# Band attention with each tile's transposes behind the next tile's scores, two key buffers in the first differential part, and row factors sent through DRAM

## The chip, the cores and the metric

The kernel runs on one core of a Trainium2 chip. A core has a matrix engine (TensorE, PE in the profile; its weight loads are listed as PEld), a vector engine (VectorE, DVE), a scalar engine (ScalarE, ACT), a general engine (GpSimd, POOL) and a queue engine (SyncE, SP) that issues all of this kernel's DMAs. Each engine takes its instructions in order; they wait for each other through semaphores. Matrix products are written to PSUM, of which this kernel uses eight banks; everything else on the core lies in SBUF, and DRAM holds inputs, outputs and scratch. The metric is the device time of one execution in microseconds, as a median of several runs.

## The reference

One inference step of a one-layer encoder for 2048 prompt tokens and 32 sample tokens, width 1024. What matters here:

```python
z = rmsnorm(x, g_attn) @ w_in             # columns: qa ka va | qb kb vb
# group A: 4 heads, differential, two maps of 64 dims each, 128-wide values
s = q·k / 8 + t5_bias,  masked by 64-token chunks
w = softmax(s_map0) - lam * softmax(s_map1);   oa = w @ v
# group B: 8 heads of 64; a 64-token chunk sees itself and the 8 chunks before it
s = q·k / 8 + clip_bias;   ob = softmax(s) @ v
h = x + concat(rmsnorm(oa) * (1 - lam_init), rmsnorm(ob)) @ w_out
h = h + relu(rmsnorm(h) @ w_up)**2 @ w_down
y = rmsnorm(h + sigmoid(h @ w_ple_gate) * (p @ w_ple_proj))
```

The keys and values of both groups are outputs too. The sample tokens run the same layer against caches of 128 rows.

## The kernel before

Products are made from numbers split in a high and a low part of a short float type (`split`), three matmuls for one product in `mm3` (lines 215 to 217). Tokens go in four blocks `b` of 512 (the last has the 32 sample tokens as well), and blocks in two halves, 0 and 1, 2 and 3.

*Preparation.* `prep` takes a block in tiles of 128 tokens: load, sum of squares on ScalarE, eight transposes into two PSUM tiles `xp`, copies out of them into the high and low activations, a copy `xt` that is written to DRAM as `xT`, and the row factor 1/rms (`rsqrt`, into one column of `rcol`). The activations are not multiplied by that factor; it is applied to the products. The value projection needs it per partition (`rcol`, line 421). The query and key projections have tokens along the free axis, so they need it as a row that is the same on all partitions: `rb[b]`, tile name `rbt`. Lines 390 to 392 make it for each tile, by a transpose of the broadcast column into a PSUM tile `rp` and a copy by ScalarE. `rp` takes its PSUM buffer from the same small rings as `xp` and, for blocks 2 and 3, as the projections (`mm`, two buffers).

*Projection.* `proj` makes values (`vtile`), then for each head group queries and keys, and writes them to DRAM scratch (`qS`, `kS`, `vS`). Lines 475 and 480 read `rb`.

*Differential attention.* `attn_a(js, ...)` runs over four heads; for a head it loads the bias tile `ba`, the keys `kt` (tile name `ka`) and then for each pair `j` of query tiles calls `attn_a_pair`, which loads queries, makes the scores (line 632), exponentials, transposes (704) and products with values (718 to 720). It is used twice: for blocks 0 and 1 (`self.small`, pool `a0`), where `ka` has one buffer of 1024 columns, and later for blocks 2 and 3, where it has two.

*Band attention.* `attn_b(js, ...)` runs over eight heads and is called for four groups of pairs: (0,1), (2,3), (4,5) and (6,7,8), pair 8 being the sample tokens. A head's bias `bb`, keys `kbt`, queries `q` and values `vbt` are loaded first. `attn_b_pair` then does, for each of the pair's two tiles of 128 queries: scores into PSUM tiles `sb` (line 802, up to 640 keys, in two pieces where there are more than 512), bias and running maximum on VectorE into `eb` (805, four buffers), exponential with its sum (810) and scaling (812) on ScalarE, transposes into `tpb` (817), and copies into a high and a low part `pHb` (826, ScalarE) and `pLb` (827, VectorE). After both tiles come the products with the values `ob` (842), two copies (846, 847) and, once a head, a store to `oT`.

*What sets the order.* The kernel is written with a tile framework that simulates the program and from it lays out one order for each engine:

```python
with tile.TileContext(nc, schedule_with_timeline_sim=True) as tc:
```

Among the instructions that are ready in that simulation, and whose buffers are free, the one that stands first in the program is taken. An instruction far down the program may thus run early where those before it wait; on the chip the order is then fixed. `lifted` gives the preparation of blocks 2 and 3 the rank of the place where the first differential part begins. In `run` the order of the parts is: preparation of blocks 0 and 1 with group A's values, group A's queries and keys for that half, `attn_a` for blocks 0 and 1, group B's projections for blocks 0 and 1 with the preparation of block 2, `attn_b` for pairs 0 to 3, group B's projections for block 2 with the preparation of block 3, and for block 3, `attn_b` for pairs 4 to 8, and then the second half of group A, output projection and MLP.

Of the kernel before, what the change touches and what calls it, by code (L numbers as in the profile page):

```python
# [15 lines left out]
ALU = mybir.AluOpType  # L16
# [126 lines left out]
class Kern:  # L143
# [214 lines left out]
    def prep(self, b, acts, pp, mm, tag, first=None):  # L358
        nc = self.nc
        aH, aL = acts[b]  # L360
        for i, (c0, n) in enumerate(toks(b)):
            t0 = 512 * b + c0
            x = pp.tile([P, D], F32, tag="x", name="x")
            self.dma(x[:n], self.xsrc(t0, n))
            if first is not None:
                first()
                first = None
            xt = pp.tile([P, 8, P], F32, tag="xt", name="xt")
            st = pp.tile([P, 1], F32, tag="st", name="st")
            nc.scalar.activation(  # L370
                xt[:n].rearrange("p a b -> p (a b)"), x[:n], AF.Square, accum_out=st[:n]
            )
            for h in range(2):
                xp = mm.tile([P, 4, P], F32, tag=tag, name="xp")
                for k in range(4):
                    kk = 4 * h + k
                    nc.tensor.transpose(xp[:, k, :n], x[:n, kk * P : kk * P + P], self.ident[:n, :n])
                for k in range(4):
                    kk = 4 * h + k
                    g = self.g_attn[:, kk : kk + 1]  # L380
                    hi, lo = aH[:, kk, c0 : c0 + n], aL[:, kk, c0 : c0 + n]
# [4 lines left out]
                nc.vector.tensor_copy(xt[:, 4 * h : 4 * h + 4, :n], xp[:, :, :n])  # L386
# [4 lines left out]
            nc.tensor.transpose(rp[:, :n], r.broadcast_to([n, P]), self.ident[:n, :n])  # L391
            nc.scalar.activation(self.rb[b][:, c0 : c0 + n], rp[:, :n], AF.Copy)
            yield

    def ktok(self, b):
# [374 lines left out]
    def attn_b_pair(self, h, j, kt, v, kb, bb, q, t1, pool, ps_s, ps_t, ps_o):  # L770
        nc = self.nc
        samp = j is None
        if samp:
# [4 lines left out]
        pH = pool.tile([P, 6, 256], F32R, tag="pH", bufs=2, name="pHb")  # L778
        pL = pool.tile([P, 6, 256], F32R, tag="pL", bufs=2, name="pLb")
        spans = []  # L780
        for qi, t in enumerate(tiles):
            if samp:
                nr, k0, n, b0 = SS, SP, PAST + SS, 384
                kts = [(0, P), (1, SS)]
            else:
                nr = P
                f = max(0, t - 4)
                k0, n = P * f, P * (t + 1 - f)
                b0 = 640 - n
                kts = [(i, P) for i in range(f, t + 1)]  # L790
            spans.append(kts)
            if n <= 512:
                nb, w = 1, n
            else:
                nb, w = 2, n // 2
            e = pool.tile([P, 640], F32, tag="e", bufs=4, name="eb")[:nr, :n]
            st = pool.tile([P, 5], F32, tag="st", bufs=4, name="stb")[:nr]
            for i in range(nb):
                s = ps_s.tile([P, 512], F32, tag="s", name="sb")[:nr, :w]
                for hl in range(2):  # L800
                    c = k0 - kb + w * i
                    nc.tensor.matmul(
                        s, q[:, hl, P * qi : P * qi + nr], kt[:, c : c + w], start=hl == 0, stop=hl == 1
                    )
                nc.vector.tensor_tensor_reduce(
                    e[:, w * i : w * i + w], s, bb[:nr, b0 + w * i : b0 + w * i + w], 1.0, -3e38,
                    ALU.add, ALU.max, st[:, 3 + i : 4 + i],
                )
            nc.vector.tensor_reduce(st[:, 0:1], st[:, 3 : 3 + nb], axis=AX.X, op=ALU.max, negate=True)
            nc.scalar.activation(e, e, AF.Exp, bias=st[:, 0:1], accum_out=st[:, 1:2])  # L810
            nc.vector.reciprocal(st[:, 2:3], st[:, 1:2])
            nc.scalar.activation(e, e, AF.Copy, scale=st[:, 2:3])
            for x0 in range(0, len(kts), 4):
                ch = kts[x0 : x0 + 4]
                tp = ps_t.tile([P, 4, P], F32, tag="tp", name="tpb")
                for x, (i, kn) in enumerate(ch):
                    nc.tensor.transpose(  # L817
                        tp[:kn, x, :nr], e[:, P * (x0 + x) : P * (x0 + x) + kn], self.ident[:nr, :nr]
                    )
                groups = [(0, len(ch), P)] if not samp else [(0, 1, P), (1, 1, SS)]  # L820
                for a0, na, kn in groups:
                    sl = ch[0][0] - kfirst + a0
                    h_ = pH[:kn, sl : sl + na, P * qi : P * qi + nr]
                    l_ = pL[:kn, sl : sl + na, P * qi : P * qi + nr]
                    s_ = tp[:kn, a0 : a0 + na, :nr]
                    nc.scalar.activation(h_, s_, AF.Copy)
                    nc.vector.tensor_tensor(l_, s_, h_.bitcast(F32), op=ALU.subtract)
        o = ps_o.tile([P, 256], F32, tag="o", name="ob")
        order = []
        if samp:  # L830
            order = [(0, P, 0, nq), (1, SS, 0, nq)]
        else:
# [5 lines left out]
            order += [(i, P, 128, 256) for i in s1 if i not in s0]  # L838
        for x, (i, kn, qa, qb) in enumerate(order):
            vt = v[:kn, (SP - kb) // P + i] if samp else v[:kn, i - kb // P]  # L840
            for y, pt in enumerate((pH, pL)):
                nc.tensor.matmul(  # L842
                    o[:, qa:qb], vt, pt[:kn, i - kfirst, qa:qb],
                    start=x == 0 and y == 0, stop=x == len(order) - 1 and y == 1,
# [725 lines left out]
```

## Time and profile before

| | us |
|---|---|
| median of 3 runs | 3191.57 (3189.75 to 3192.46) |
| the profiled execution | 3197.78 |
| its span, first to last instruction | 3196.0 |
| TensorE busy in the span | 3037.6 |
| ScalarE, GpSimd, VectorE busy | 1885.5, 1887.4, 1851.6 |
| mean granted TensorE clock | 0.977 |

A line of a group of instructions names the source line, the engine, the operation and the tiles written and read, then how often it ran, its busy time, the mean duration of one, and the idle time of the engine before it with what ended it. A line of a wait reads "engine, tile, line <- what it waited for: total us, times, longest". A line of a timeline starts with the time from the span's start and the duration; brackets hold the idle time before it and its releaser. A stage's line has its time, then busy time and number of instructions of PE, PEld, DVE, ACT and POOL, the granted clock, the DMA engines' mean busy share and their rate. Busy times of matmuls include overlap in the pipeline, so that the distance from start to start says what one costs in a row of many.

### The profile page before, as it was taken

To read this page: it belongs to the slowest core of one execution; us is meant where nothing else is said; L and a number is where in the kernel's file an instruction comes from. 1 tells how busy PE (TensorE), PEld (TensorE's weight loads), DVE (VectorE), ACT (ScalarE), POOL (GpSimd) and SP (SyncE) were. 2 spreads that over 40 slices of the span, in tenths; PEclk is the share of its full clock that TensorE was granted. 3 is DMA by queue.
4 is the path that set the end of the run, shared out by engine and by line. 5 is a ranking of instruction groups with operands and counts; after the bars stand their busy time and mean duration, and the time that the engine had idled before them with its cause. 6 is when DMAs were issued, how large, how long until landed. Compare 5 with 4: busy or idle time off the path is not lost.

```text
span 3196.0 us, 53414 instructions
## 1 busy us (share of the span) xinstructions
PE 3037.6 (95%) x18265; PEld 2694.5 (84%) x18265; DVE 1851.6 (58%) x4448; ACT 1885.5 (59%) x4166; POOL 1887.4 (59%) x2572
## 2 busy tenths in 40 slices
PE   8998989999999998999999999998999999899998
PEld 7787877899987787877788888877888888899998
DVE  5157774544454554666765666435577665776663
ACT  5256775766665764676665666554555555554445
POOL 4466546333335544565554555677787778867674
PEclk9998999999999999999999999999999999999999
DMA  8787767977688745555554534446524334233331
GB/s 267 237 242 224 208 191 237 251 227 206 199 244 227 209 130 134 149 165 138 170 158 139 148 111 119 126 147 216 182 86 147 106 99 127 93 100 108 92 114 55
DMA packets 512505, 521.61 MB, mean 163 GB/s; under 512 B 37949, under 2 KB 393601, under 8 KB 512233
## 3 DMA queue, kind: packets, MB, share of 16 engines
q1 hardware_dynamic: 512232, 518.19, 55.2%
q8 instruction: 145, 2.38, 0.3%
q14 instruction: 128, 1.04, 0.1%
HBM read 412.08 MB, written 109.95 MB: 163 GB/s over the span
## 4 chain that ended last, share of the span: by engine, by line
PE 68%; DMA 12%; DVE 10%; ACT 4%; issue 3%; POOL 2%; SPq 1%; DVEq 0%; ACTq 0%; POOLq 0%
PE dps L215 6%; PE dps L216 6%; PE dps L217 6%; PE ups L215 6%; PE ups L216 6%; PE ups L217 6%; PE s L632 3%; PE qps L215 3%; PE qps L216 3%; PE qps L217 3%; DMA oraw<-oT 2%; PE ob L842 2%; PE tpb L817 1%; PE tpp L704 1%; DMA wr<-w_up 1%
## 5 line engine op out<-in xcount | busy, mean ns | idle before, releaser
L175 POOL TENSOR_TENSOR wl<-wr,wh 128x256 fp32r<-128x256 f32 x648 | 474.5, 764 | 333.6 <-ACT wh L180 328.0
L180 ACT ACTIVATE piece<-wr 128x512 fp32r<-128x512 f32 x412 | 252.9, 626 | 289.0 <-PE ups L216 144.0
L175 POOL TENSOR_TENSOR piece<-wr,piece 128x256 fp32r<-128x256 f32 x416 | 336.4, 834 | 103.2 <-ACT piece L180 87.8
L180 ACT ACTIVATE wh<-wr 128x1024 fp32r<-128x1024 f32 x228 | 240.8, 1057 | 198.5 <-PE qps L216 51.7
L165 POOL TENSOR_TENSOR wl<-wr,wh 128x256 fp32r<-128x256 f32 x264 | 197.9, 781 | 185.8 <-ACT wh L180 180.4
L215 PE MATMUL ups<-cs,piece 128*128 128x256 f32 (+1 forms) x896 | 257.3, 288 | 7.8 <-ACT piece L180 6.1
L217 PE MATMUL ups<-cs,piece 128*128 128x256 f32 (+1 forms) x896 | 257.4, 287 | 5.6 <-POOL piece L175 5.6
L216 PE MATMUL ups<-cs,piece 128*128 128x256 f32 (+1 forms) x896 | 256.6, 286 | 0.5 <-DVE cs L186 0.5
L216 PE MATMUL dps<-ul,piece 128*128 128x272 f32 (+1 forms) x768 | 247.7, 324 | 1.3 <-DVE ul L186 1.3
L217 PE MATMUL dps<-uh,piece 128*128 128x272 f32 (+1 forms) x768 | 247.5, 324 | 1.2 <-POOL piece L165 1.2
L215 PE MATMUL dps<-uh,piece 128*128 128x272 f32 (+1 forms) x768 | 246.2, 324 | 1.0 <-DVE h L1124 0.8
L165 POOL TENSOR_TENSOR piece<-wr,piece 128x256 fp32r<-128x256 f32 x280 | 223.5, 829 | 25.1 <-ACT piece L180 24.3
L1124 DVE TENSOR_TENSOR h<-h,dps 128x272 f32<-128x272 f32 (+1 forms) x384 | 190.8, 515 | 81.5 <-PE dps L217 80.5
L215 PE MATMUL qps<-aH,wh 128*128 128x512 f32 (+1 forms) x640 | 230.8, 361 | 5.8 <-DVE ql L475 4.3
L215 PE MATMUL dps<-uh,wh 128*128 128x512 f32 x512 | 209.5, 409 | 20.8 <-ACT wh L180 7.2
L216 PE MATMUL qps<-aL,wh 128*128 128x512 f32 (+1 forms) x640 | 229.2, 358 | 0.0
L217 PE MATMUL qps<-aH,wl 128*128 128x512 f32 (+1 forms) x640 | 228.4, 357 | 0.0
L1083 DVE TENSOR_TENSOR h<-h,dps 128x512 f32<-128x512 f32 x256 | 174.2, 682 | 82.3 <-PE dps L217 77.6
L632 PE MATMUL s<-ka,q 128*128 128x512 f32 (+3 forms) x768 | 188.6, 349 | 19.4 <-DMA ka<-kS 10.0
L215 PE MATMUL ups<-cH,wh 128*128 128x512 f32 x512 | 202.7, 396 | 0.5 <-DVE h L1083 0.4
L216 PE MATMUL dps<-ul,wh 128*128 128x512 f32 x512 | 202.1, 395 | 0.0
L217 PE MATMUL dps<-uh,wl 128*128 128x512 f32 x512 | 202.1, 395 | 0.0
(298 smaller groups left out, 9764.7 us busy)
## 6 DMA issues: line engine op xcount, KB each, us to landing
wr<-w_up SPq DMA_DIRECT2D x128, 512.0 KB, 4.1
wr<-w_down SPq DMA_DIRECT2D x128, 512.0 KB, 3.7
wr<-w_in SPq DMA_DIRECT2D x74, 512.0 KB, 4.6
q<-qS SPq DMA_DIRECT2D x128, 256.0 KB, 5.2
v<-vSa SPq DMA_DIRECT2D x64, 512.0 KB, 3.9
ka<-kS SPq DMA_DIRECT2D x32, 512.0 KB, 7.8
wr<-w_out SPq DMA_DIRECT2D x32, 512.0 KB, 5.0
wr<-w_ple_gate SPq DMA_DIRECT2D x32, 512.0 KB, 4.1
```

The costliest lines, as they stand in the source:

```text
L165: nc.gpsimd.tensor_tensor(out[:, sl], a[:, sl], b[:, sl], op=op)
L175: nc.gpsimd.tensor_tensor(out[:, sl], a[:, sl], b[:, sl], op=op)
L180: nc.scalar.activation(hi, raw, AF.Copy)
L215: nc.tensor.matmul(ps, lh, rh, start=start and i == 0, stop=False)
L216: nc.tensor.matmul(ps, lh, rl, start=False, stop=False)
L217: nc.tensor.matmul(ps, ll, rh, start=False, stop=stop and i == n - 1)
L632: nc.tensor.matmul(s, q[:, m, hl, P * qi : P * qi + nr], kt[:, m, k0 - kb : k0 - kb + n], start=hl == 0, stop=hl == 1)
L704: nc.tensor.transpose(tp[:kn, x, :nr], w[:nr, P * i : P * i + kn], self.ident[:nr, :nr])
L817: nc.tensor.transpose(tp[:kn, x, :nr], e[:, P * (x0 + x) : P * (x0 + x) + kn], self.ident[:nr, :nr])
L842: nc.tensor.matmul(o[:, qa:qb], vt, pt[:kn, i - kfirst, qa:qb], start=x == 0 and y == 0, stop=x == len(order) - 1 and y == 1,)
L1083: nc.vector.tensor_tensor(hv, hv, ps, op=ALU.add)
L1124: nc.vector.tensor_tensor(hv, hv, ps, op=ALU.add)
```

## The change

Three edits.

*Row factors.* The transpose and the copy for each tile go. After the last tile of a block its four columns of `rcol` are written to a DRAM row `rR` (for block 3 the sample tokens' column too), and one DMA reads the row back into `rb[b]`, broadcast to all partitions.

*Keys of the first differential part.* `ka` gets two buffers there as well.

*Band attention.* `attn_b_pair` no longer makes a tile from scores to copies at one go. A function `first` holds the scores, the bias, the exponential and the scaling; `second` the transposes and the two copies and, for the pair's last tile, the products with the values (now `attn_b_out`). `step` runs a tile's `first` and then the `second` that was left over from the tile before, also across pairs and heads; the very last is run at the end of the call. `tc.issue_after(ins)` puts an edge from `ins`, the last score matmul of the new tile, to every TensorE instruction traced in the block, so that these stand behind it in TensorE's order; it adds no semaphore. The store to `oT` is chained to the `second` of the head's last tile.

```diff
+        self.rR = self.dram([T], F32, "rR")
...
-            rp = mm.tile([P, 512], F32, tag=tag, name="rp")
-            nc.tensor.transpose(rp[:, :n], r.broadcast_to([n, P]), self.ident[:n, :n])
-            nc.scalar.activation(self.rb[b][:, c0 : c0 + n], rp[:, :n], AF.Copy)
+            if i == len(toks(b)) - 1:
+                self.dma(
+                    self.rR[512 * b : 512 * b + 512].rearrange("(i p) -> p i", p=P), self.rcol[:, 4 * b : 4 * b + 4]
+                )
+                if b == 3:
+                    self.dma(self.rR[SP:T].rearrange("(i p) -> p i", p=SS), self.rcol[:SS, 16:17])
+                self.dma(
+                    self.rb[b][:, : BN[b]],
+                    self.rR[512 * b : 512 * b + BN[b]].unsqueeze(0).broadcast_to([P, BN[b]]),
+                )
...
-            kt = pool.tile([P, 2, 1024 if self.small else SP], F32R, tag="ka", bufs=1 if self.small else 2, name="ka")
+            kt = pool.tile([P, 2, 1024 if self.small else SP], F32R, tag="ka", bufs=2, name="ka")
...
+        late = []
+
+        def step(first):
+            ins = first()
+            if late:
+                with self.tc.issue_after(ins):
+                    late.pop(0)()
...
                 self.attn_b_pair(
-                    h, j if j < 8 else None, kt, v, kb, bb, qs[x], tt[:, 256 * x : 256 * x + nq], pool, ps_s, ps_t, ps_o
+                    h, j if j < 8 else None, kt, v, kb, bb, qs[x], tt[:, 256 * x : 256 * x + nq], pool, ps_s, ps_t, ps_o,
+                    step, late,
                 )
             t0, n = 256 * js[0], 256 * (len(js) - 1) + nq
-            self.dma(self.oT[64 * m : 64 * m + 64, gi, t0 : t0 + n], tt[:, :n])
...
+            late.append(self.then(late.pop(), lambda m=m, gi=gi, tt=tt, t0=t0, n=n: self.dma(
+                self.oT[64 * m : 64 * m + 64, gi, t0 : t0 + n], tt[:, :n]
+            )))
+        late.pop(0)()
...
+            def first(qi=qi, nr=nr, k0=k0, n=n, b0=b0, nb=nb, w=w, held=held):
+                e = pool.tile([P, 640], F32, tag="e", bufs=4, name="eb")[:nr, :n]
...
+                    for hl in range(2):
+                        c = k0 - kb + w * i
+                        ins = nc.tensor.matmul(
+                            s, q[:, hl, P * qi : P * qi + nr], kt[:, c : c + w], start=hl == 0, stop=hl == 1
+                        )
...
+                nc.scalar.activation(e, e, AF.Exp, bias=st[:, 0:1], accum_out=st[:, 1:2])
+                nc.vector.reciprocal(st[:, 2:3], st[:, 1:2])
+                nc.scalar.activation(e, e, AF.Copy, scale=st[:, 2:3])
+                return ins.ins
+
+            def second(qi=qi, nr=nr, kts=kts, held=held, end=t is tiles[-1]):
+                if qi == 0:
+                    for x in ("pHb", "pLb"):
+                        px.append(pool.tile([P, 6, 256], F32R, tag=x[:2], bufs=2, name=x))
...
+                    for x, (i, kn) in enumerate(ch):
+                        nc.tensor.transpose(
+                            tp[:kn, x, :nr], e[:, P * (x0 + x) : P * (x0 + x) + kn], self.ident[:nr, :nr]
+                        )
...
+                        nc.scalar.activation(h_, s_, AF.Copy)
+                        nc.vector.tensor_tensor(l_, s_, h_.bitcast(F32), op=ALU.subtract)
+                if end:
+                    self.attn_b_out(samp, nq, spans, kfirst, kb, v, px, t1, ps_o)
+
+            step(first)
+            late.append(second)
```

More of the change, by code (lines that the diff above doesn't have):

```diff
@@ L777, in attn_b_pair @@
         kfirst = 0 if samp else max(0, 2 * j - 4)
-        pH = pool.tile([P, 6, 256], F32R, tag="pH", bufs=2, name="pHb")
-        pL = pool.tile([P, 6, 256], F32R, tag="pL", bufs=2, name="pLb")
+        px = []
         spans = []
@@ L795, in attn_b_pair @@
                 nb, w = 2, n // 2
[L796 to L803, printed above, removed]
-                    )
[L805 to L827, printed above, removed]
@@ new lines, in attn_b_pair @@
+            held = []
+            def first(qi=qi, nr=nr, k0=k0, n=n, b0=b0, nb=nb, w=w, held=held):
+                e = pool.tile([P, 640], F32, tag="e", bufs=4, name="eb")[:nr, :n]
+                st = pool.tile([P, 5], F32, tag="st", bufs=4, name="stb")[:nr]
+                held.append(e)
+                for i in range(nb):
+                    s = ps_s.tile([P, 512], F32, tag="s", name="sb")[:nr, :w]
+                    for hl in range(2):
[3 more added lines that the diff above has]
+                        )
+                    nc.vector.tensor_tensor_reduce(
+                        e[:, w * i : w * i + w], s, bb[:nr, b0 + w * i : b0 + w * i + w], 1.0, -3e38,
+                        ALU.add, ALU.max, st[:, 3 + i : 4 + i],
+                    )
+                nc.vector.tensor_reduce(st[:, 0:1], st[:, 3 : 3 + nb], axis=AX.X, op=ALU.max, negate=True)
+                nc.scalar.activation(e, e, AF.Exp, bias=st[:, 0:1], accum_out=st[:, 1:2])
+                nc.vector.reciprocal(st[:, 2:3], st[:, 1:2])
+                nc.scalar.activation(e, e, AF.Copy, scale=st[:, 2:3])
+                return ins.ins
@@ new lines, in second @@
+            def second(qi=qi, nr=nr, kts=kts, held=held, end=t is tiles[-1]):
+                if qi == 0:
+                    for x in ("pHb", "pLb"):
+                        px.append(pool.tile([P, 6, 256], F32R, tag=x[:2], bufs=2, name=x))
+                pH, pL = px
+                e = held[0]
+                for x0 in range(0, len(kts), 4):
+                    ch = kts[x0 : x0 + 4]
+                    tp = ps_t.tile([P, 4, P], F32, tag="tp", name="tpb")
+                    for x, (i, kn) in enumerate(ch):
+                        nc.tensor.transpose(
+                            tp[:kn, x, :nr], e[:, P * (x0 + x) : P * (x0 + x) + kn], self.ident[:nr, :nr]
+                        )
+                    groups = [(0, len(ch), P)] if not samp else [(0, 1, P), (1, 1, SS)]
+                    for a0, na, kn in groups:
+                        sl = ch[0][0] - kfirst + a0
+                        h_ = pH[:kn, sl : sl + na, P * qi : P * qi + nr]
+                        l_ = pL[:kn, sl : sl + na, P * qi : P * qi + nr]
+                        s_ = tp[:kn, a0 : a0 + na, :nr]
+                        nc.scalar.activation(h_, s_, AF.Copy)
+                        nc.vector.tensor_tensor(l_, s_, h_.bitcast(F32), op=ALU.subtract)
+                if end:
+                    self.attn_b_out(samp, nq, spans, kfirst, kb, v, px, t1, ps_o)
@@ L840, in attn_b_pair @@
             vt = v[:kn, (SP - kb) // P + i] if samp else v[:kn, i - kb // P]
-            for y, pt in enumerate((pH, pL)):
+            for y, pt in enumerate(px):
                 nc.tensor.matmul(
```

10 lines of the change are left out of this document (8 added, 2 removed).

## The prediction

> **What bounds the kernel now.** I read the page first (busy time and the chain that ended last), then the busy time by stage, then what TensorE itself waited for, and last the timelines around those waits. From the page:
>
> ```profile
> span 3196.0 us, 53414 instructions
> ...
> PE 3037.6 (95%) x18265; PEld 2694.5 (84%) x18265; DVE 1851.6 (58%) x4448; ACT 1885.5 (59%) x4166; POOL 1887.4 (59%) x2572
> ...
> PE 68%; DMA 12%; DVE 10%; ACT 4%; issue 3%; POOL 2%; SPq 1%; DVEq 0%; ACTq 0%; POOLq 0%
> ```
>
> TensorE is the bound. The stages that the change touches are the first differential part with the projections woven into it (184 to 520 us) and the band part (520 to 1240):
>
> ```profile
> core 0: us, PE busy (x) PEld busy (x) DVE busy (x) ACT busy (x) POOL busy (x), PEclk, DMA share, GB/s
> 184.00:520.00 336.00, 301.19 (x1788) 267.62 (x1787) 227.95 (x719) 231.35 (x668) 205.79 (x297) 0.92 0.74 213
> 520.00:1240.00 720.00, 691.01 (x4435) 620.85 (x4434) 358.45 (x1242) 471.06 (x990) 318.69 (x491) 0.99 0.73 208
> 1240.00:3196.00 1956.00, 1880.40 (x11101) 1666.19 (x11100) 1203.82 (x2319) 1109.22 (x2324) 1286.26 (x1672) 0.98 0.44 130
> ```
>
> The first stage idles 34.8 us of 336 and has a granted clock of 0.92; the band idles 29.0 us of 720 at 0.99; behind both, TensorE is busy 96% of the time. So a microsecond of TensorE idling that goes in the first two stages should come off the end nearly whole: projection work from further down the program fills in wherever the plan lets it. Only idle time and the clock can be won; the matmuls stay, but for 17. What TensorE waited for, over the whole run (total, times, longest):
>
> ```profile
> PE sb L802 <- DVE stb L805: 11.5, 11, 2.4
> PE s L632 <- DMA ka<-kS: 10.0, 4, 3.8
> PE ob L842 <- ACT pHb L826: 7.2, 7, 2.3
> ...
> PE rp L391 <- DVE xt L386: 7.1, 6, 2.1
> ...
> PE rp L391 <- DVE rcol L230: 2.0, 3, 1.1
> ```
>
> Each part of the change has its row here: the key loads 10.0, the row-factor transposes 9.1, the band 18.7. These 37.8 us are what is at stake directly. An idle stretch costs more than itself, as TensorE's timeline round the longest key wait shows:
>
> ```profile
> 293.46 1.62 PE L632 MATMUL s<-ka,q 128*128 128x384 f32 x4 [3.78 <-DMA ka<-kS]
> ...
> 296.16 0.41 PE L216 MATMUL vps<-wl,aH 128*128 128x256 f32 x1
> 296.37 0.41 PE L217 MATMUL vps<-wh,aL 128*128 128x256 f32 x1
> ...
> 298.79 0.28 PE L217 MATMUL vps<-wh,aL 128*128 128x256 f32 x1
> 298.90 0.28 PE L215 MATMUL vps<-wh,aH 128*128 128x256 f32 x1
> ```
>
> After the wait equal matmuls start 0.21 us apart, and by 298.79 us 0.11 us apart: about 5 us ran at half rate, a further loss of 2.5 us behind a wait of 3.78.
>
> **The second key buffer (8 heads).** Nothing is added but 8 KB a partition; the loads are the same bytes, allowed to start a head earlier. SyncE's timeline at that head change, and the loads' sizes and median times to landing:
>
> ```profile
> 279.64 0.59 SPq L156 DMA_DIRECT2D ka<-kS  x1
> ...
> 282.42 1.35 SPq L156 DMA_DIRECT2D q<-qS  x2
> ```
>
> ```profile
> q<-qS SPq DMA_DIRECT2D x128, 256.0 KB, 5.2
> ...
> ka<-kS SPq DMA_DIRECT2D x32, 512.0 KB, 7.8
> ```
>
> With one buffer the load cannot be issued before the last score matmul of the head before, and 7.8 us is longer than what the plan has to put in between. With two it has the length of a whole head, so the wait goes. Next late are the query loads of the same head, issued behind the keys (5.2 us, two buffers, so they may start one pair earlier), and the bias tile, which keeps one buffer. Upper end: all 10.0 us, plus the half-rate stretches behind the three long waits, an estimate of 2 us each from the 2.5 above: 16. Lower end: the query load ends at the same time and nothing is won; below that, earlier key bursts push value loads back, which I bound by one key wait, -3.8. I take half of the upper end, 8 us.
>
> The Trainium skill ("TensorE: Matmul & The Clock Gate", Part 1) says that the clock gate falls to half after an idle window of about 3.4 us and needs a busy one to rise; the 3.78 us wait and the half-rate matmuls behind it agree. By that rule a wait that is only shortened below a window gives back its half-rate stretch as well, which would make the term 16 rather than 8.
>
> **The row factors through DRAM.** Seventeen transposes go, with their copies on ScalarE:
>
> ```profile
> L391 PEld LDWEIGHTS rp<-ident,rcol x17: 127/133/183, 10.7 to 526.1; 128*128 128x128 f32 x16, 32*128 32x128 f32 x1
> L391 PE MATMUL rp<-ident,rcol x17: 237/323/477, 10.7 to 526.1; 128*128 128x128 f32 x16, 32*128 32x32 f32 x1
> L392 ACT ACTIVATE rbt<-rp x17: 188/277/313, 11.9 to 526.4; 128x128 f32<-128x128 f32 x16, 128x32 f32<-128x32 f32 x1
> ```
>
> ```profile
> 526.05 0.24 PE L391 MATMUL rp<-ident,rcol 32*128 32x32 f32 x1 [2.10 <-DVE xt L386]
> 526.62 0.50 PE L215 MATMUL qps<-aH,wh 128*128 128x512 f32 x1 [0.33 <-ACT rbt L392]
> ```
>
> The 2.10 us are not won: the transpose waited for a PSUM buffer that VectorE's copy had to free, and the projection matmul behind it would wait for the same buffer. What goes is the 0.57 us from the one to the other. So per tile between 0.13 us (the weight load alone) and 0.57: 2.3 to 9.7 us for 17. I take 5, nearer the lower end for the half of them that stand among dense matmuls. The 4.7 us (17 x 0.277) on ScalarE are worth nothing, it is 69% busy in that stage.
>
> Added on SyncE: five writes of 4-byte pieces and four reads that fan one row out to 128 partitions. The nearest rows are the output norm's factors, written and read back the same way (first two lines), and a load of 4-byte pieces (last two):
>
> ```profile
> L156 SPq DMA_DIRECT2D rb<-rB x4: 320/405/3437, 917.2 to 2086.4; - x4
> ...
> DMA to landing us min/median/max: 2.6/5.1/8.3
> ```
>
> ```profile
> L156 SPq DMA_DIRECT2D g_mlp_s<-g_mlp x1: 435/435/435, 4.4 to 4.4; - x1
> ...
> DMA to landing us min/median/max: 6.4/6.4/6.4
> ```
>
> A round trip is 0.4 + 6.4 + 0.4 + 5.1 = 12.3 us. It is hidden if the factors are used later than that; VectorE's timeline has the last factor of the first half and the first product that reads any of them:
>
> ```profile
> 54.69 0.16 DVE L230 TENSOR_TENSOR rcol<-rsy,rsv 128x1 f32<-128x1 f32 x1
> ...
> 76.10 0.69 DVE L475 SCALAR_TENSOR_TENSOR ql<-qps,rbt 128x512 f32<-128x512 f32 x1
> ```
>
> There are 21.4 us, and blocks 2 and 3 use theirs still later, so latency costs nothing. The queue may: SyncE issues in order, the write waits for the tile's last factor, and the read waits for the write. One rb read held SyncE for 3.4 us (the maximum above); four such are 13.7 us in which weight and input loads stand behind. They are covered while two raw weight buffers are ahead; if that cover is gone, the 13.7 us are the price. I take 0.
>
> **The band order.** Transposes of a tile and the value products of a pair now stand behind the next tile's score matmuls in the program, and an edge keeps that order on TensorE. The planner has it already. TensorE's timeline in the middle of the band, and who VectorE waits for there:
>
> ```profile
> 690.81 0.97 PE L802 MATMUL sb<-kbt,q 128*128 128x320 f32 x4 [0.75 <-DVE stb L805]
> 691.91 0.74 PE L817 MATMUL tpb<-ident,eb 128*128 128x128 f32 x5
> ...
> 693.24 0.97 PE L802 MATMUL sb<-kbt,q 128*128 128x320 f32 x4 [0.27 <-DVE stb L805]
> ...
> 698.07 0.73 PE L817 MATMUL tpb<-ident,eb 128*128 128x128 f32 x5
> ```
>
> ```profile
> DVE eb L805 <- PE tpb L817: 61.9, 51, 3.2
> ```
>
> Transposes start 0.13 us after scores end, far too soon to be the same tile's (the exponential and the scaling lie between). VectorE takes scores only when an old probability tile is freed by its transposes: scores already run up to four tiles ahead, the limit of the four e buffers. So the edge binds almost nowhere, not even at a head change, where the transposes will stand behind scores that need new keys. Only priorities shift: bias adds, exponentials and scalings of tile t+1 now rank before the copies of tile t. The band's stores to oT move behind the next head's six loads on SyncE; they are read only by the norms much later, and their tile has two buffers, so I count 0. The 18.7 us of waits are the upper end; at the other end they grow (the slower rival). Neither row is near; since both kinds of wait come from a plan that misjudges VectorE and ScalarE, I take 4 us.
>
> **Sum.** 8 + 5 + 4 = 17 us. The profiled execution took 3197.78 us, 1.8 more than its span and 6.2 above the median of the runs; 17 off it is 3180.8, off the median of 3191.57 it is 3174.6, which I forecast as 3174.
>
> **The rivals.** *Slower: value products wait for ScalarE.* ScalarE's work for a band tile, from the groups of the band's window:
>
> ```profile
> L810 ACT ACTIVATE eb<-eb,stb 128x640 f32<-128x640 f32 (+5 forms) x136 | 100.4, 739 | 48.9 <-DVE stb L809 47.1 <-POOL wl L175 1.2
> L812 ACT ACTIVATE eb<-eb,stb 128x640 f32<-128x640 f32 (+5 forms) x136 | 99.5, 737 | 16.0 <-DVE stb L811 16.0
> ```
>
> With the new ranks 0.74 + 0.74 = 1.5 us of the next tile can stand before the copy that a pair's products need, and those hold TensorE's queue. If that shows as 0.6 us of idling in each of the 72 pairs it costs 43 us: 3191.6 - 13 + 43 = 3222, less with filler, so 3215. It decides from 0.18 us a pair (13/72), against 0.10 now (7.2/72). For it: this wait is already the band's second largest, and a changed program order makes a whole new plan. Against: TensorE has projection matmuls to put there, and the plan accounts for ScalarE.
>
> *No change: one wait takes another's place.* Query loads and bias tiles follow the keys, the PSUM buffer follows the transposes, SyncE's holds eat the rest: 17 - 13.7 leaves 3 us, 3188; the band does nothing since its order stood.
>
> *More: the clock comes back too.* Terms of 16, 10 and 13 (two thirds of the band's waits): 39 us, 3152.
>
> **How the numbers follow.** The forecast's case has 0.45 (own range 3160 to 3184), more 0.15, no change 0.10, slower 0.30. Within 0.2% is 6.4 us either way, about what a measurement of this kernel can tell. So faster 0.60, same 0.10, slower 0.30. The range runs from 3147, past the case of more, to 3222, the slower one's time without filler.
>
> **What would show it.** Right: no wait of s on ka between 184 and 520 us, that stage's clock above 0.92, no L391 and L392, rows of factors landing long before L475 reads them, and TensorE's waits on pHb and stb not above their 18.7 us. Wrong: waits on q, ba or e in place of ka; SyncE held at the factor reads with wr late behind them; ob <- pHb above 20 us in the band; or a band that ends later although no single wait grew, because filler was planned elsewhere.

## The result and the profile after

The kernel became slower: 3215.49 us as a median of four runs (3212.73 to 3218.51), 3192.02 for the kernel before on the same chip. The ratio of the two is 1.0064 (95% interval 1.0047 to 1.0082), some 20 us (the medians differ by 23.5), where 17 us less was forecast. The profiled execution took 3212.73 us. From its page, as for the kernel before, the busy time by engine and the chain that ended last:

```profile
span 3210.7 us, 53385 instructions
...
PE 3040.8 (95%) x18248; PEld 2694.5 (84%) x18248; DVE 1846.9 (58%) x4448; ACT 1883.7 (59%) x4149; POOL 1887.3 (59%) x2572
...
PE 66%; DMA 13%; DVE 10%; ACT 4%; POOL 3%; issue 3%; SPq 1%; DVEq 0%; POOLq 0%; ACTq 0%
```

The seventeen matmuls are gone, TensorE is as busy as before, and the chain looks the same. The page alone doesn't show the loss; the list of what TensorE waited for does (total, times, longest):

```profile
PE vps L215 <- ACT vraw L429: 19.5, 7, 8.7
PE tpp L712 <- DVE e L677: 14.3, 6, 5.0
PE xp L378 <- DVE kr L488: 11.4, 1, 11.4
PE s L640 <- DVE nm L649: 8.0, 8, 3.0
...
PE sb L832 <- DVE stb L835: 5.5, 5, 3.3
...
PE ob L887 <- ACT pHb L864: 1.0, 2, 0.6
```

The three rows that the prediction set out to remove (`s` on `ka`, `rp`, and most of the band's) are indeed gone; of the band's 18.7 us, 5.5 and 1.0 are left. At the top stand waits of the value projection and the preparation; the longest are 8.7 and 11.4 us in one piece, and both of these begin soon after a row-factor write. The busy times by stretches of 8 us in the first 90 us, after (the last two columns are the DMA engines' share and their rate in GB/s):

```profile
32.00:40.00 8.00, 7.49 (x65) 7.29 (x64) 3.64 (x10) 3.00 (x10) 2.72 (x4) 1.00 1.04 123
...
56.00:64.00 8.00, 7.49 (x66) 7.18 (x65) 4.47 (x16) 3.97 (x13) 2.21 (x3) 1.00 0.82 188
64.00:72.00 8.00, 1.74 (x16) 1.54 (x14) 0.00 (x0) 0.00 (x0) 0.00 (x0) 0.80 1.13 26
72.00:80.00 8.00, 5.58 (x30) 5.58 (x31) 2.85 (x8) 1.45 (x4) 2.18 (x3) 0.56 0.90 276
```

and the same view of before:

```profile
32.00:40.00 8.00, 8.00 (x73) 8.00 (x72) 5.84 (x15) 6.50 (x21) 5.70 (x9) 1.00 1.04 318
...
64.00:72.00 8.00, 8.00 (x66) 7.70 (x65) 1.19 (x4) 1.43 (x3) 2.21 (x3) 1.00 0.53 172
```

From 64 to 72 us the DMA engines are listed as fully busy (1.13) and move 26 GB/s. VectorE, ScalarE and GpSimd do nothing at all. SyncE's timeline says what was issued just before:

```profile
60.03 0.40 SPq L156 DMA_DIRECT2D rR<-rcol  x1
...
62.77 0.62 SPq L156 DMA_DIRECT2D vSa<-vhl  x1
72.87 0.32 SPq L156 DMA_DIRECT2D rbt<-rR  x1
73.28 0.38 SPq L156 DMA_DIRECT2D va_p<-vraw  x1
```

The write of 512 factors starts at 60.0, the read that waits for it is issued at 72.9, and in between SyncE issues nothing for 9.5 us. One can follow the wait upwards through the timelines of VectorE, ScalarE and TensorE:

```profile
72.70 0.29 DVE L182 CAST vhl<-vraw 128x256 fp32r<-128x256 f32 x1 [11.64 <-DMA vSa<-vhl]
```

```profile
73.29 0.37 ACT L383 ACTIVATE aH<-xp,g_attn_s 128x128 fp32r<-128x128 f32 x1 [10.72 <-DVE aL L384]
```

```profile
74.42 0.58 PE L215 MATMUL vps<-wh,aH 128*128 128x256 f32 x1 [8.68 <-ACT vraw L429]
```

VectorE waits for a buffer of `vhl` whose store to `vSa` does not finish, ScalarE waits for VectorE, TensorE for ScalarE. It isn't the row factor that is late for anyone; it is a store that has nothing to do with it. In the last block the victim is a cache load, by SyncE's timeline issued 3.2 us after the write and not there before 519.6:

```profile
506.19 0.38 SPq L156 DMA_DIRECT2D rR<-rcol  x1
...
509.34 0.42 SPq L156 DMA_DIRECT2D cvr<-cache_b_v  x1
```

```profile
519.61 0.29 DVE L182 CAST cvhl<-cvr 128x256 fp32r<-128x256 f32 x1 [13.45 <-DMA cvr<-cache_b_v]
519.82 0.68 DVE L488 TENSOR_TENSOR kr<-qps,rbt 128x512 f32<-128x512 f32 x1
```

This one stands in VectorE's queue ahead of `kr` (line 488), which frees the PSUM buffer for `xp`: the wait of 11.4 us. How the loss builds up can be read off the first and the last score matmul (the two times behind the durations are the first and the last start of the group), after:

```profile
L640 PE MATMUL s<-ka,q x768: 219/337/796, 193.5 to 2024.3; 128*128 128x256 f32 x68, 128*128 128x384 f32 x64, 128*128 128x512 f32 x52, 128*128 128x128 f32 x8
```

against before:

```profile
L632 PE MATMUL s<-ka,q x768: 220/338/797, 184.7 to 2010.2; 128*128 128x256 f32 x68, 128*128 128x384 f32 x64, 128*128 128x512 f32 x52, 128*128 128x128 f32 x8
```

8.8 us are lost before the first score, and 14.1 by the last one, which is nearly the whole difference of the spans (14.7).

The stages of the prediction, after:

```profile
184.00:520.00 336.00, 289.53 (x1767) 255.03 (x1765) 216.59 (x705) 222.36 (x647) 197.00 (x287) 0.94 0.75 209
520.00:1240.00 720.00, 688.43 (x4413) 619.69 (x4414) 360.01 (x1252) 471.39 (x995) 316.05 (x490) 0.97 0.75 212
```

The clock of the first rose from 0.92 to 0.94, as predicted, yet TensorE is busy 11.7 us less there (301.19 before). In the band it is busy 2.6 us less. The bounds are the same clock times in both kernels, so part of this is the work that arrives 8.8 us later.

So theory A is that the small-piece writes stall the DMA engines, and the rest of the change is harmless. Theory B is that the new band order, or the new plan it makes, costs the time; theory C is that no part costs anything alone and they only disturb each other.

### The profile page after: what moved, and what is told of

Its sections match the earlier page's. It is cut to its first block, busy times and chain, and to the rows that moved or that the text cites. A ratio compares the mean times of both kernels' runs of the same rounds, so it can differ in the third digit from the quotient of the medians.

```text
span 3210.7 us, 53385 instructions
## 1 busy us (share of the span) xinstructions
PE 3040.8 (95%) x18248; PEld 2694.5 (84%) x18248; DVE 1846.9 (58%) x4448; ACT 1883.7 (59%) x4149; POOL 1887.3 (59%) x2572
## 4 chain that ended last, share of the span: by engine, by line
PE 66%; DMA 13%; DVE 10%; ACT 4%; POOL 3%; issue 3%; SPq 1%; DVEq 0%; POOLq 0%; ACTq 0%
PE dps L215 6%; PE dps L216 6%; PE dps L217 6%; PE ups L215 6%; PE ups L217 6%; PE ups L216 6%; PE qps L215 2%; PE s L640 2%; PE qps L217 2%; PE qps L216 2%; DMA oraw<-oT 2%; PE ob L887 2%; PE tpb L855 2%; DMA wr<-w_up 2%; PE sb L832 2%
## 5 line engine op out<-in xcount | busy, mean ns | idle before, releaser
L215 PE MATMUL dps<-uh,wh 128*128 128x512 f32 x512 | 209.5, 409 | 11.7 <-DVE h L1128 6.1
```

Of the source, the lines that this page charges most:

```text
L215: nc.tensor.matmul(ps, lh, rh, start=start and i == 0, stop=False)
```

## The experiments

**Which part.** Four kernels: the change without its row factors, and each part alone.

```diff
 # e1: keys and band; e2: row factors; e3: keys; e4: band, each on the kernel before
-            kt = pool.tile([P, 2, 1024 if self.small else SP], F32R, tag="ka", bufs=1 if self.small else 2, name="ka")
+            kt = pool.tile([P, 2, 1024 if self.small else SP], F32R, tag="ka", bufs=2, name="ka")   # e1, e3
...
-            rp = mm.tile([P, 512], F32, tag=tag, name="rp")
...
+            if i == len(toks(b)) - 1:
+                self.dma(self.rR[...].rearrange("(i p) -> p i", p=P), self.rcol[:, 4 * b : 4 * b + 4])   # e2
...
+        late = []                        # e1, e4: step, first, second as in the change
```

> The change without its row-factor part: the transposes of the factors stay, nothing goes through DRAM. Theory A (the five writes of 4-byte pieces and the reads behind them hold SyncE's queue and the DMA engines, and that costs more than the other two parts win): the loss is gone and the predicted 8 + 4 us of the other parts show, 3180 us (3172 to 3188); the first query projection starts near 70 us again instead of 86. Theory B (the new order of the band, or the new plan of the whole that it makes, costs the time): 3205 us or more, near the changed kernel's 3215. Theory C (no part costs anything alone, the parts disturb each other): between, 3188 to 3200.

> The kernel before with the row factors through DRAM and nothing else. A: slower than before by more than the whole change is, since the gains of the other parts are missing: 3192 + 23.5 + 12 = 3227 us (3212 to 3235), lost in the first 90 us and round the fourth block. B: 3192 - 5 = 3187 us, as the prediction had this part (within 5 us of the kernel before at worst). C: 3192 to 3200.

> The kernel before with the second key buffer and nothing else. A and B both: no wait of the scores on the keys between 184 and 535 us, and 3192 - 8 = 3184 us (3176 to 3192) as the prediction had this part. C: same time as before, within 3 us, the wait moved to the query loads, the bias tile or the probability copies.

> The kernel before with the band's new order and nothing else. A: 3192 - 4 = 3188 us (3182 to 3194), the band's waits on pHb and stb smaller, as in the changed kernel. B: 3205 to 3220 us, with the loss outside the band's own waits, in a plan that puts its filler elsewhere. C: within 3 us of the kernel before.

| | ratio to before | 95% interval |
|---|---|---|
| whole change | 1.0064 | 1.0047 to 1.0082 |
| e1 keys and band | 0.9991 | 0.9978 to 1.0004 |
| e2 row factors alone | 1.0127 | 1.0108 to 1.0145 |
| e3 keys alone | 1.0009 | 0.9999 to 1.0018 |
| e4 band alone | 1.0006 | 0.9996 to 1.0016 |

The row factors are the loss, some 40 us when alone (0.0127 x 3192). B falls: three kernels with wholly new plans all lie within 0.1% of before, so without the write the plan's chance is no larger than that. But A's numbers for the gains were wrong too: keys and band are worth nothing that can be measured. For the keys, TensorE's waits between 184 and 535 us show why. In the kernel before these were

```profile
PE s L632 <- DMA ka<-kS: 10.0, 4, 3.8
PE rp L391 <- DVE xt L386: 6.6, 5, 2.1
PE s L632 <- ACT e L646: 3.8, 4, 1.8
...
PE s L632 <- DVE nm L641: 0.5, 2, 0.3
```

and with two key buffers

```profile
PE s L632 <- ACT e L646: 8.2, 9, 2.6
PE rp L391 <- DVE xt L386: 7.5, 4, 3.8
PE s L632 <- DVE nm L641: 6.3, 4, 3.0
```

The 10.0 us on the keys are gone, the scores now wait for the probability buffers and the maxima instead: 4.4 and 5.8 us more.

The smaller waits of the band in the changed kernel are not the work of the band's new order either. Of the 18.7 us in its two rows 16.5 stay with the new order alone (e4: 9.6 and 6.9) and 6.5 with the second key buffer alone (e3: 4.8 and 1.7). Yet e3, which lost them, is no faster, and e8 below, which has both edits, keeps 14.9. They differ from plan to plan, and no run shows that the time follows them.

**What in the row part.** There are three suspects: the write stalls the DMA engines (clog), its reader holds SyncE's queue (hold), the factors come a block late. Four kernels. In e5 the transposes stay and the five writes are added, which nobody reads; in e6 each is made twice; e7 and e8 turn a block's factors into rows by one transpose, so that a write has 4 pieces of 512 bytes, e7 on the kernel before and e8 with the other two parts.

```diff
 # e5 (e6: once more into a second buffer)
             rp = mm.tile([P, 512], F32, tag=tag, name="rp")
 ...
+            if i == len(toks(b)) - 1:
+                self.dma(self.rR[512 * b : 512 * b + 512].rearrange("(i p) -> p i", p=P), self.rcol[:, 4 * b : 4 * b + 4])
```

```diff
 # e7, e8: the write of the changed kernel (the sample tokens' row goes the same way)
-                self.dma(self.rR[512 * b : 512 * b + 512].rearrange("(i p) -> p i", p=P), self.rcol[:, 4 * b : 4 * b + 4])
+                rp = mm.tile([P, 512], F32, tag=tag, name="rp")
+                nc.tensor.transpose(rp[:4, :P], self.rcol[:, 4 * b : 4 * b + 4], self.ident)
...
+                nc.scalar.activation(rw[:, :P], rp[:4, :P], AF.Copy)
+                self.dma(self.rR[512 * b : 512 * b + 512].rearrange("(i p) -> i p", p=P), rw[:, :P])
...
```

> The kernel before, transposes and all, with the five writes of 4-byte pieces added; nobody reads what they write, so no read and no factor waits for them. Clog theory (a write of 512 pieces of 4 bytes keeps the DMA engines from other transfers for some 8 to 12 us): most of the row part's loss is here, ratio 1.006 to 1.012, with a gap of 5 us or more on TensorE near 70 us and another near 515 us. Hold theory (the writes are cheap, the read that waits for them on SyncE's queue holds the loads behind it): ratio 0.999 to 1.002. Late-factor theory (the products wait for factors that come a block later): also 0.999 to 1.002.

> As the kernel with the unread writes, each write made twice, the second to another buffer that nobody reads. Clog theory: the loss about doubles, ratio 1.012 to 1.024, both gaps twice as long. Hold theory and late-factor theory: 0.999 to 1.003, as with one write.

> The kernel before with the row factors through DRAM, but each block's factors are first turned into rows by one transpose (and one of 32 factors more in the last block), so that a write has 4 pieces of 512 bytes instead of 512 of 4; the reads are the same. Clog theory: the loss is gone, ratio 0.998 to 1.001 (13 transposes and copies fewer than before, worth 2 to 5 us at most). Hold theory: SyncE still waits for every write before its read, two thirds of the loss stay, 1.008 or more. Late-factor theory: all of it stays, 1.010 to 1.014.

> The changed kernel with such long-piece writes in place of its own: two key buffers, the band's new order, row factors through DRAM without the small pieces. Clog theory: the best of what the change can give, 0.997 to 1.000 of the kernel before. Hold theory and late-factor theory: 1.004 to 1.008, near the changed kernel's 1.006.

| | ratio to before | 95% interval |
|---|---|---|
| e5 writes, unread | 1.0088 | 1.0071 to 1.0104 |
| e6 the same twice | 1.0115 | 1.0098 to 1.0133 |
| e7 long rows alone | 0.9980 | 0.9970 to 0.9991 |
| e8 long rows, keys, band | 0.9982 | 0.9971 to 0.9994 |

Writes that nobody reads cost 28 us (0.0088 x 3192). A read or a late factor can't be the reason there. e7 keeps the round trip and is 6 us faster than before; SyncE still waits for the write before its read, but 4.3 us in all where it waits 30.0 in e2. So the clog is shown, and hold and late factor on their own are not the cause: behind a quick write they cost nothing visible. What a read costs that holds SyncE behind a slow write is not shown by e7, since a quick write shortens both. In e5 even the issue of later stores is held up, as SyncE's timeline shows (start, time of the issue; two stores take 8.67 us; in e11, below, a single one takes 6.48):

```profile
30.24 0.37 SPq L156 DMA_DIRECT2D rR<-rcol  x1
...
34.43 8.67 SPq L156 DMA_DIRECT2D vSa<-vhl  x2
```

The dose failed: twice the pieces cost 1.3 times the loss, not 2. The stretch without transfers didn't get longer. Busy times in that stretch, e6:

```profile
64.00:66.00 2.00, 2.00 (x19) 2.00 (x19) 1.21 (x4) 1.08 (x4) 0.74 (x1) 1.00 0.88 132
66.00:72.00 6.00, 6.00 (x55) 6.00 (x54) 1.08 (x3) 0.85 (x2) 0.00 (x0) 1.00 0.00 0
```

and e5:

```profile
66.00:72.00 6.00, 6.00 (x55) 6.00 (x55) 1.50 (x4) 0.85 (x3) 0.78 (x2) 1.00 1.17 42
72.00:74.00 2.00, 1.34 (x12) 1.14 (x11) 0.00 (x0) 0.00 (x0) 0.00 (x0) 1.00 0.61 11
```

So it isn't the number of pieces as such, and the next four kernels ask what it is.

**What in the write.** All are the kernel before with unread writes.

```diff
 # e9: one column of the four (no sample tokens)
+                self.dma(self.rR[512 * b : 512 * b + P].rearrange("(i p) -> p i", p=P), self.rcol[:, 4 * b : 4 * b + 1])
 # e10: rR is [T, 128], each piece 512 bytes from the next; e13: [T, 16], 64 bytes
+                self.dma(self.rR[512 * b : 512 * b + 512, 0].rearrange("(i p) -> p i", p=P), self.rcol[:, 4 * b : 4 * b + 4])
 # e11: as e5, on ScalarE's queue
+                nc.scalar.dma_start(self.rR[...].rearrange("(i p) -> p i", p=P), self.rcol[:, 4 * b : 4 * b + 4])
 # e12: a partition's four factors side by side (no sample tokens)
+                self.dma(self.rR[512 * b : 512 * b + 512].rearrange("(p i) -> p i", p=P), self.rcol[:, 4 * b : 4 * b + 4])
```

> The kernel before with unread writes again, but only one column of 128 factors per block: 128 pieces of 4 bytes in place of 512. If the stall goes with the number of pieces: a quarter of the loss of the unread writes (1.009), 1.001 to 1.004. If each small-piece write costs a stall of its own whatever its size (two at once cost little more than one): 1.006 to 1.010 again.

> Unread writes of 512 pieces of 4 bytes as before, but each piece to a place 512 bytes from the next, so no two pieces lie in one 512-byte stretch of DRAM. If pieces that share a stretch of DRAM wait for each other (the clog is one of neighbours): the stall goes, 0.999 to 1.003. If the number of pieces alone makes the clog: 1.007 to 1.011, and again 8 us of low transfer rate behind each write.

> The same unread writes, of 512 adjacent pieces, issued by ScalarE on its own queue instead of SyncE. If the stall is in SyncE's queue (transfers behind the write wait in order): most of the loss goes, 1.000 to 1.004, and SyncE's transfers keep over 200 GB/s beside the write. If the 16 DMA engines or the memory behind them are stopped: 1.006 to 1.012, and the rate falls below 100 GB/s as before.

> The same unread bytes, but each partition's four factors side by side, so 128 pieces of 16 bytes per block, adjacent in DRAM. If the number of pieces counts: as with one column, 1.001 to 1.004. If adjacency in DRAM counts (32 pieces to a 512-byte stretch in place of 128): some loss, 1.003 to 1.007. If every write costs its own stall: 1.006 to 1.010.

> Unread writes of 512 pieces of 4 bytes, each piece 64 bytes from the next (16 times the distance of the changed kernel's, an eighth of the 512 bytes that cost nothing). If pieces stall each other only within the same few bytes: 0.999 to 1.002, as at 512. If they do so within a 512-byte stretch: the eight pieces in each stretch give some loss, 1.001 to 1.004 (between 32 pieces of 16 bytes to a stretch, 1.0012, and none).

The landing times are the medians, from issue to landing, of the row of DMA issues that each kernel's trace has for this write.

| | pieces a block | to landing, us | ratio | 95% interval |
|---|---|---|---|---|
| e5 adjacent | 512 of 4 bytes | 11.4 | 1.0088 | 1.0071 to 1.0104 |
| e9 adjacent, one column | 128 of 4 | 10.7 | 1.0079 | 1.0067 to 1.0091 |
| e11 adjacent, ScalarE's queue | 512 of 4 | 12.6 | 1.0104 | 1.0089 to 1.0118 |
| e12 adjacent | 128 of 16 | 2.1 | 1.0012 | 1.0002 to 1.0022 |
| e13 64 bytes apart | 512 of 4 | 2.9 | 1.0010 | 0.9999 to 1.0021 |
| e10 512 bytes apart | 512 of 4 | 3.0 | 0.9995 | 0.9983 to 1.0006 |

The row for e9 reads

```profile
rR<-rcol SPq DMA_DIRECT2D x4, 0.5 KB, 10.7
```

and for e10

```profile
rR<-rcol SPq DMA_DIRECT2D x4, 2.0 KB, 3.0
```

Four times the bytes in four times the pieces land in under a third of the time once the pieces lie apart. From e5 to e10 nothing in the edit differs but the distance: the same 512 pieces of 4 bytes, issued from the same line. In e10 the second block's write is issued at 55.4 us, and in the eight microseconds behind it TensorE is busy throughout while the DMA engines move 199 GB/s:

```profile
56.00:64.00 8.00, 8.00 (x73) 8.00 (x72) 4.09 (x13) 3.92 (x13) 2.21 (x3) 1.00 0.63 199
```

So the small pieces are not the cause; 4-byte pieces next to each other are. Being adjacent isn't enough by itself: e12's 128 adjacent pieces of 16 bytes land after 2.1 us and cost 1.0012, below the 1.003 to 1.007 that was expected if adjacency counts. It fits with e6 and e9 that 128 neighbours (one column, one stretch of 512 bytes) take as long as four or eight such stretches: as if the pieces of one stretch went one after the other and the stretches side by side. e12, with 32 pieces to such a stretch, doesn't speak against it. That is a reading of the times, no run looked into the memory. How wide the stretch is stays open: 64 bytes between pieces is already enough (e13).

Another queue doesn't help. In e11 SyncE has nothing to do with the write, and the engines still stop; busy times, e11:

```profile
60.00:62.00 2.00, 2.00 (x20) 2.00 (x19) 0.53 (x3) 0.97 (x3) 0.05 (x1) 1.00 0.89 280
62.00:70.00 8.00, 5.67 (x50) 5.46 (x49) 0.83 (x3) 1.47 (x4) 0.69 (x1) 1.00 0.06 1
```

280 GB/s fall to 1 GB/s for 8 us. The Trainium skill ("DMA: Bandwidth & Descriptors", Rules for kernel authors) says that spreading DMAs over several issuing engines gives no bandwidth, since they run on the same 16 DMA engines; the trace agrees in so far as the write on ScalarE's queue stops the transfers that SyncE issued. The same page of the Trainium skill (Specifications) gives 512 bytes as the least transfer for full rate, with a read-modify-write below it. By that alone e10 and e13 would have paid as e5 did; their 3.0 and 2.9 us to landing say that here the distance decides, so this rule of the Trainium skill alone doesn't tell the changed kernel's write from theirs.

**Why the whole is better than its worst part.** The row part alone has 1.0127, keys and band 0.9991, and together they make 1.0064, not 1.012. Two kernels, each leaving one part out:

```diff
 # e14: row factors and two key buffers, the band in its old order (the edits of e2 and e3 together)
 # e15: row factors and the band's new order, one key buffer
-            kt = pool.tile([P, 2, 1024 if self.small else SP], F32R, tag="ka", bufs=2, name="ka")   # e15
+            kt = pool.tile([P, 2, 1024 if self.small else SP], F32R, tag="ka", bufs=1 if self.small else 2, name="ka")
```

> The row factors through DRAM and the second key buffer, the band in its old order. If the key buffers take back half of the row part's loss (a stalled key load then has a whole head to land): 1.005 to 1.008, as the whole change. If the band's order does it: 1.011 to 1.014, as the row part alone. If it is a chance of the plan: anything between, and the next run too.

> The row factors through DRAM and the band's new order, one key buffer. If the key buffers take back half of the loss: 1.011 to 1.014, as the row part alone. If the band's order does it (the row part alone has waits of 3 to 4 us in the band that the whole change has not): 1.005 to 1.008.

e14 measured 1.0068 (1.0056 to 1.0081), e15 1.0106 (1.0091 to 1.0122). The key buffers take half of the loss back: from e2 to e14 it is 0.59% of the time, and with the band's new order, from e15 to the whole change, 0.42%. (e15 lies just under the 1.011 to 1.014 that was expected for this case.) The band's order gives 0.21% (e2 to e15) and 0.04% (e14 to the whole), neither clear of the intervals. One would look for that in the first differential part, where these loads are; but up to 560 us TensorE has done nearly the same work in both (from 184 to 560 us it is busy 323.7 us in e2 and 325.0 in e14). They part in the stretch behind it, where the first band pairs and group B's projections run. Busy times there, e2:

```profile
560.00:800.00 240.00, 220.00 (x1687) 213.43 (x1688) 111.67 (x447) 157.97 (x361) 92.27 (x153) 0.95 0.81 228
```

and e14:

```profile
560.00:800.00 240.00, 231.09 (x1800) 223.26 (x1799) 115.00 (x455) 166.91 (x368) 101.08 (x164) 0.99 0.82 233
```

11 us more of work at a clock of 0.99 rather than 0.95. What TensorE waits for in that stretch of e2 and hardly or not at all in e14:

```profile
PE sb L810 <- DVE stb L813: 4.3, 1, 4.3
PE ktp L520 <- DVE ql L483: 4.2, 2, 2.9
PE qps L215 <- ACT kn L513: 4.0, 1, 4.0
PE sb L810 <- DMA q<-qS: 3.7, 2, 2.4
```

These are few and long, and the first and last of them hold band scores. Where the loss is taken back is shown by that; why the key buffers spare the band these waits isn't. No stalled write lies in that stretch (the last one of e2 is issued at 538.7 us), so the order that the planner chose for it is a likelier reason than the loads, but that wasn't tried.

## Why the prediction was wrong

**The step that failed is the price of the added DMAs, "latency costs nothing ... I take 0".** The unread writes measured 28 us, the row part as a whole 40. The change loses 20 us although its keys take part of that back. The error has three layers.

The nearest row was misread. The prediction took "the output norm's factors, written and read back the same way". The read is the same; the write isn't, as the DMA issues of before list it (count, KB each, median to landing):

```profile
rB<-r SPq DMA_DIRECT2D x3, 256.0 KB, 6.2
rb<-rB SPq DMA_DIRECT2D x3, 256.0 KB, 4.9
```

A write of 256 KB is a 128 x 512 tile in long rows; the factors are 2 KB. No 4-byte *store* stood in the trace, and a 4-byte load (6.4 us) was put in its place. The store of 512 adjacent pieces lands after 11.4 us in e5, up to 12.8 in the changed kernel. On its own that wouldn't have mattered: with 3.7 us for the read (the median in the changed kernel) it stays within the slack of 21.4.

The price was sought with the reader. The prediction compared the round trip with the time until `ql` reads the factors, and that comparison holds: no wait on `rbt` is among the costly ones. What costs is every other transfer under way. The bound at the other end, 13.7 us of SyncE's holds, was too small as well. It counted the time that the reads take to issue and not the wait for the write ahead of them: that wait is 29.4 us in the changed kernel, and the unread writes, where nobody waits so, cost 28. Between e2 and e5 lie another 12 us, although e2 is spared the transposes; the read that holds SyncE behind a slow write may be that rest, but it is a difference of two kernels with plans of their own, and no run shows it apart.

And the cover was named for the wrong transfers. "Two raw weight buffers are ahead" speaks of weight loads. The ones that were late were stores of values and a cache load, with two buffers each, and through their buffers VectorE and ScalarE stood still.

**The transposes (5 us) came out as forecast, as far as a run can show it.** With long pieces the round trip gives 0.9980, 6.4 us less (0.0020 x 3192; the interval is 2.9 to 9.6), with 12 transposes fewer than before rather than 17. That agrees with the term, though not as the change wrote it. e1, e3 and e4, with plans of their own, lie up to 0.1% from the kernel before, so the transposes' own share in the 6.4 us is not shown.

**The second key buffer (8 us) was wrong in a kernel without the stall, by the rival "one wait takes another's place".** The predicted wait went, 10.0 to nothing. Named as next late were query loads and bias tile; in fact it was the probability buffer and the maxima (10.2 us more together), that is ScalarE and VectorE. The upper end of 16 was built on waits that would vanish; the lower end, "nothing is won", is what was measured (1.0009). In the kernel with the stalling writes it is worth 0.6% (e2 to e14), mostly outside the stage that it was meant for. The idea that a wait that is only shortened gives its whole half-rate stretch back isn't borne out either: in the kernel before, the granted clock was 0.50 from 1078 to 1080 us, and the longest waits just ahead of that were 1.10 and 1.48 us.

**The band order (4 us): 1.0006, no difference.** "The edge binds almost nowhere" fits that, and so do the 16.5 us of waits that e4 keeps; taking 4 us from a plan expected to differ by chance was one-sided.

**The slower rival had the sign and the wrong place.** It wanted products waiting for ScalarE in the band, `ob` on `pHb` above 20 us. That wait is 1.0 us over the whole run of the changed kernel. The 3215 it gave is the measured time by coincidence, and it is by this rival's upper end that the range held the result. Of what the prediction listed as signs of being wrong, two came: SyncE held at the factor reads, which was listed and priced at 0, and, with the second key buffer alone, waits on `e` in place of `ka`.

**A better version.** e7 and e8 beat both kernels, by 0.20% and 0.18% against before. Keys and band add nothing to it: e8 and e7 can't be told apart. What the change has to offer is the row factors in long pieces.

## What to carry to other kernels

Before sending a column of SBUF to DRAM, ask how its pieces lie in DRAM: here 128 adjacent 4-byte pieces took 10.7 us to land, and 512 of them nearly stopped the other transfers for up to 8 us, issued from SyncE or from ScalarE. Making rows of them first with one transpose cured it (e7), and so did laying them 64 or 512 bytes apart (e13 and e10, where nobody read them back). The cost of a DMA isn't the latency to its reader alone; look at who else has transfers under way and how many buffers stand between those and the busiest engine. And a wait removed is only won if the list of waits doesn't show its time again under another name in the same stage.

## What the runs showed that was not expected

- The bytes are 0.5 KB, the time some 10 us: a write of 128 adjacent 4-byte pieces lands after 10.7 us, 512 of them 64 or 512 bytes apart after 2.9 and 3.0, and 128 of 16 bytes after 2.1.
- During it the other transfers fall from 280 to 1 GB/s (e11) and from 172 to 26 (changed kernel against before), while the listed busy share may be 1.13: a busy DMA share alone doesn't say what is moved.
- The loss grows little with the number of adjacent pieces between 128 and 1024 a block (1.0079, 1.0088, 1.0115).
- A part that is worth nothing alone (1.0009) takes back half of another part's loss (1.0127 to 1.0068), more than half of it in the stretch behind the stage that it changes.
